# A 32x32 block inverse handed on inside SBUF, instead of through DRAM

## The chip, the cores and the metric

The kernel runs on one core of a Trainium2 chip. It uses all five engines: PE (TensorE, matrix products and transposes by product), DVE (VectorE), ACT (ScalarE), POOL (GpSimd) and SP (SyncE), whose instruction queue issues nearly all transfers between DRAM and the on-chip memories SBUF and PSUM. Each engine works through its own instructions strictly in order; an instruction that waits holds up everything behind it on that engine. The metric is the device time in microseconds (us) of one execution. Before the change it is 1262.1 us, the median of 3 runs (1261.81 to 1263.61).

## The reference, cut to what matters

The program is one layer of a hybrid encoder on 2048 positions of width 1024: RMS norm, one input projection, then two groups of heads in parallel, an output projection, and the residual sum. Group A (four heads of 128) is a gated delta rule run forwards and backwards; group B is windowed attention. The change lies in group A, in the part that inverts a unit lower triangular matrix for each chunk:

```python
    m = jnp.where(strict, jnp.einsum('bhncd,bhnsd->bhncs', k_beta, k) * decay, 0.0)
    eye = jnp.eye(c, dtype=q.dtype)
    t_inv = lax.linalg.triangular_solve(eye + m, jnp.broadcast_to(eye, m.shape),
                                        left_side=True, lower=True, unit_diagonal=True)
    u = jnp.einsum('bhncs,bhnse->bhnce', t_inv, v * beta[..., None])
    w = jnp.einsum('bhncs,bhnsd->bhncd', t_inv, k_beta * jnp.exp(g)[..., None])
    ...
    _, o = lax.scan(step, state0, xs)
```

The scan over chunks needs the inverses and is sequential: each step's state comes from the one before. The kernel uses chunks of 128 positions (16 per head and direction) instead of 64, which gives the same result by another split.

## The kernel before, in words

The first half of the program (up to some 690 us) makes the projections, the convolutions and the attention. The second half, `phase_b`, takes the four delta-rule heads one after another, and overlaps head h's scan with the preparation of head h+1:

- `pre_front(h)` makes, for all 16 chunks and both directions, the matrices m (with a product gh on PE, line 702, and a scaling on DVE into the tiles ma, line 711; for some heads these tiles lie in memory called xhi_h and xlo_h). Each group of four chunks is stored to DRAM (m_d, line 716). The memory of ma comes free only as earlier scans end: the front of head 2 ends behind the last steps of scan 0, that of head 3 behind those of scan 1. So from solve on, three pieces overlap: scan h, solve h+1, and then the end of front h+2.
- `solve(h)` reads back from m_d the 32x32 blocks on the diagonals (tiles X and L, lines 739 and 740): 2 directions x 16 chunks x 4 blocks are 128 blocks, one per SBUF partition, each with 32x32 numbers in the row. It inverts all of them at once by 31 steps of two DVE instructions (lines 749 and 753), and stores the result X to DRAM (x_d, line 754).
- `invert(h)` builds the 128x128 inverses from the block inverses, in four rounds `hi` of four chunks forwards and four backwards. For each round it loads two tiles xc from x_d (line 765): there a chunk's 128 rows lie on 128 partitions, with 4 chunks x 32 columns in the row. DVE transposes each 32x32 block of xc into xt (line 766); small copies place the blocks into block-diagonal tiles, iv (line 776, on DVE in round 0 and on DVE and POOL in the later ones) and ma (line 793, POOL). Then come five products on PE (pi, line 781) with ACT copies between.
- `scan(h)` is the sequential part: 16 steps for each of two directions, each with products pk, py, po on PE, copies on ACT and sums S, r, oacc on DVE.
- `fill` takes units of the output projection of group B (products pcs, lines 596 to 598) as work that depends on little and may stand anywhere in this half.

The order in which each engine runs its instructions is not that of the source text. At the end, `set_order` builds the graph of all instructions with a cost for each, plans it forwards and backwards several times, and pins the order of each engine's queue to the plan with the earliest planned end. So a change anywhere may move instructions everywhere. Tiles are taken from pools with a number of buffers: xc and xt have four each, L and X one each.

Of the kernel before, what the change touches and what calls it, by code (L numbers as in the profile page):

```python
# [7 lines left out]
F32 = mybir.dt.float32  # L8
F32R = mybir.dt.float32r
AF = mybir.ActivationFunctionType  # L10
# [5 lines left out]
P = 128  # L16
# [3 lines left out]
NCH = 16  # L20
# [526 lines left out]
def phase_b(ctx, wide, xe, ae, late, tc, t, ident, consts, hp, mix_dn, mix_sw, kq_d, v_d, zdn_d, zsw_d, dp, out):  # L547
    nc = tc.nc
    V, A, G, T = nc.vector, nc.scalar, nc.gpsimd, nc.tensor
    dma = nc.sync.dma_start  # L550

    def pool(name, bufs=1, stack=ctx, **kw):
        return stack.enter_context(tc.tile_pool(name=name, bufs=bufs, reuse_waits="tile", **kw))
# [63 lines left out]
    qa = pool("qa", stack=pre_stack)  # L617
# [5 lines left out]
    quads = [slice(32 * p, 32 * p + 32) for p in range(4)]  # L623
# [17 lines left out]
    def pre_front(h):  # L641
        H = {}
# [7 lines left out]
        mp = {}  # L650
        ma = H["ma"] = {}
        m_d = dp.tile([2, NCH, 4 * (32 * P + 32)], F32, tag="m_d", name=f"m_d{h}", bufs=2)
        x_d = dp.tile([2, NCH, P, 32], F32, tag="x_d", name=f"x_d{h}", bufs=2)
        for n, c4 in enumerate(FRONT):
            s4 = slice(4 * c4, 4 * c4 + 4)
            cs = slice(c4 * 512, (c4 + 1) * 512)
# [5 lines left out]
            for d in range(2):  # L662
# [12 lines left out]
                p = 3 - c4 if d else c4  # L675
# [22 lines left out]
            for c2 in range(2):  # L698
                gh = ps_g.tile([P, 2, 2, P], F32, tag="gh", name=f"gh{h}_{c4}_{c2}")
                for k in range(2):  # L700
                    c = 2 * c2 + k
# [3 lines left out]
                for k in range(2):  # L705
                    c = 2 * c2 + k
# [20 lines left out]
        for d in range(2):  # L727
            V.tensor_tensor(ck[:, d], bp[:, d], ekd[:, d, :, h], ALU.mult)

        H["solve"] = m_d, x_d, mp  # L730
        return H

    def solve(h, H):
        m_d, x_d, _ = H["solve"]
        L = qa.tile([P, 32, 32], F32, tag="L", name=f"L{h}")
        X = qa.tile([P, 32, 32], F32, tag="X", name=f"X{h}")
        lv = [m_d[d].rearrange("u (p y) -> (u p) y", p=4)[:, : 32 * P] for d in range(2)]
        lv = [a.rearrange("q (r x) -> q r x", x=P)[:, :, :32] for a in lv]
        dma(X[0:64], lv[0])
        dma(L[64:128], lv[1])  # L740
        x = X.rearrange("p r c -> p (r c)")
        V.tensor_copy(L[0:64], X[0:64].rearrange("p r c -> p c r"))
        G.memset(x, 0.0)
        G.memset(x[:, ::33], 1.0)
        for c in range(31):
            n = 31 - c
            tm = qa.tile([P, 256], F32, tag="tm", name=f"tm{h}_{c}")
            tv = tm[:, : n * (c + 1)].rearrange("p (r k) -> p r k", k=c + 1)
            V.tensor_tensor(
                tv, L[:, c + 1 :, c : c + 1].to_broadcast([P, n, c + 1]),  # L750
                X[:, c : c + 1, 0 : c + 1].to_broadcast([P, n, c + 1]), ALU.mult,
            )
            V.tensor_tensor(X[:, c + 1 :, 0 : c + 1], X[:, c + 1 :, 0 : c + 1], tv, ALU.subtract)
        dma(x_d.rearrange("d u (p r) c -> (d u p) (r c)", p=4), X.rearrange("p r c -> p (r c)"))

    def invert(h, H):
        _, x_d, mp = H["solve"]
        for hi in range(4):
            e1, p2, e2, e3 = (z[hi % len(z)] for z in zts)
            m = mp[hi]  # L760
            x0, x1 = {}, {}
            for d, c4 in ((0, hi), (1, 3 - hi)):
                xc = qb.tile([P, 4, 32], F32, tag="xc", name=f"xc{h}_{d}_{c4}", bufs=4)
                xt = qb.tile([P, 4, 32], F32, tag="xt", name=f"xt{h}_{d}_{c4}", bufs=4)
                dma(xc, x_d[d, 4 * c4 : 4 * c4 + 4].rearrange("u i c -> i u c"))
                V.transpose(xt.rearrange("p u c -> p (u c)"), xc.rearrange("p u c -> p (u c)"))
                x0[d], x1[d] = (xc, xt) if d == 0 else (xt, xc)
            g = qb.tile([P, 4, P], F32, tag="g", name=f"g{h}_{hi}", bufs=2)
            G.tensor_tensor(g, m[:, :, 0], m[:, :, 1], ALU.add)
            for s, a, b in zip("VGG" if hi else "VVV", (e1, e2, e3), ([0, 1, 0, 1], [1, 0, 1, 0], [0, 0, 1, 1])):  # L770
                xs = x1 if a is e2 else x0
                for q, k in zip(quads, b):
                    if s == "A":
                        A.activation(a[q, :, q], xs[k][q], AF.Copy)
                    else:
                        (V if s == "V" else G).tensor_copy(a[q, :, q], xs[k][q])

            def prod(j, lhs, rhs):
                o = ps_i[(hi + j) % 2].tile([P, 4, P], F32, tag="inv", name=f"pi{j}_{h}_{hi}")
                for c in range(4):  # L780
                    T.matmul(o[:, c], lhs(c), rhs(c), start=True, stop=True)  # L781
                return o

            def half(c):
                a = m[:, c].rearrange("p s i -> p (s i)")[:, :384].rearrange("p (e x) -> p e x", x=192)
                return a[:, :, :64]

            o = prod(0, lambda c: g[:, c], lambda c: e1[:, c])
            b1 = qb.tile([P, 4, P], F32, tag="b1", name=f"b1{h}_{hi}", bufs=2)
            A.activation(b1, o, AF.Copy, scale=-1.0)  # L790
            for d in range(2):
                for q in quads:
                    G.tensor_copy(m[q, :, 1 - d, q], x1[d][q])
            o = prod(1, lambda c: e2[:, c], lambda c: b1[:, c])
            for q, r in ((1, 0), (2, 3)):
                A.activation(e3[quads[q], :, quads[r]], o[quads[q], :, quads[r]], AF.Copy)
            o = prod(2, lambda c: b1[:, c], lambda c: e2[:, c])
            for r, q in ((0, 1), (1, 0), (2, 3), (3, 2)):
                A.activation(m[quads[r], :, 1 - r % 2, quads[q]], o[quads[r], :, quads[q]], AF.Copy)
            o = prod(3, lambda c: g[:, c], lambda c: e3[:, c])  # L800
            for d in range(2):
                A.activation(p2[halves[1 - d], :, halves[d]], o[halves[1 - d], :, halves[d]], AF.Copy, scale=-1.0)
            o = prod(4, lambda c: p2[:, c], half)
            for d in range(2):
                A.activation(m[halves[d], :, 1 - d, halves[1 - d]], o[halves[d], :, halves[1 - d]], AF.Copy)
# [90 lines left out]
    with tc.using_default_side("right"):  # L896
        zp = pool("zp", 4, stack=wide)
    kvs = {}
    H = pre_front(0)
    late(zp)  # L900
    solve(0, H)
    zts = [[const(f"iv{j}_{i}", [P, 4, P], None, qb) for i in range(2 - j % 2)] for j in range(4)]
    for grp in zts:
        for a in grp:
            G.memset(a, 0.0)
    invert(0, H)
    e1, e2 = (xe.tile([P, 8, 4, P], F32, tag=k, name=f"{k}_h") for k in ("xhi", "xlo"))
    mas = {1: e1[:, 0:4], 2: e1[:, 4:8], 0: e2[:, 4:8]}
# [8 lines left out]
    for h in range(3):  # L917
        scan(h, H)
        H = pre_front(h + 1)
        solve(h + 1, H)  # L920
        invert(h + 1, H)
# [19 lines left out]
    with tc.high_priority(-1000000):  # L941
        for k in range(2):
# [5 lines left out]
            for p in (0, 4, 2, 6, 5, 1, 3):  # L948
# [8 lines left out]
                a = (b11, b21, b22, b21, b11, b22, b12)[p]  # L957
# [459 lines left out]
```

## Time and profile before

| | |
|---|---|
| median of 3 runs | 1262.1 us |
| profiled execution: device time | 1270.01 us |
| profiled execution: span from first to last instruction | 1268.0 us |
| mean granted PE clock over the span | 0.989 |
| PE busy | 1210.5 us, 95% of the span |
| DVE busy | 953.7 us, 75% |
| ACT busy | 725.8 us, 57% |
| POOL busy | 529.2 us, 42% |

The profiled execution is 0.6% longer than the median; a sum of differences made in the trace is set against the trace's own time and then taken off the median. The share of busy time is an average over stages with different limits, so it says little by itself: what counts is, for each stage, which engine idles and which wait ends last there. The granted clock is the share of its full speed at which PE was allowed to run; a busy PE at clock 0.5 does half the work.

### The profile page before, as it was taken

The numbers are of one execution on the slowest core, as the hardware profiler recorded it, in microseconds if no ns is written. First come the engines' busy times: TensorE is split into PE (matmuls) and PEld (weight loads), VectorE is DVE, ScalarE is ACT, GpSimd is POOL, SyncE is SP. The second block draws the span as 40 slices with busy tenths as digits, with TensorE's granted clock in tenths as the row PEclk, the third lists the DMA queues.
The fourth block names the chain that finished last, engine by engine and source line by source line (L and its number), as shares of the span: only waits on it lengthen the run. The fifth ranks groups of instructions, "written<-read, shape, count | busy, mean of one in ns | idle before, by whom it ended". The sixth has DMA issues, their size and how long they took to land.

```text
span 1268.0 us, 22351 instructions
## 1 busy us (share of the span) xinstructions
PE 1210.5 (95%) x7018; PEld 1037.4 (82%) x7018; DVE 953.7 (75%) x2320; ACT 725.8 (57%) x2167; POOL 529.2 (42%) x845
## 2 busy tenths in 40 slices
PE   6999999999999999999999998999889899999898
PEld 5998888788889988887777777888789689888776
DVE  4523689999854379999995587698769779876765
ACT  6432476666534367766665438658557845685421
POOL 2243454763302276556422304613742441670541
PEclk9999999999999999999999999999889999999999
DMA  7553243513544434431016848967955875854785
GB/s 259 172 160 125 75 154 100 173 60 102 166 145 125 144 110 137 137 96 55 34 51 207 238 141 245 264 189 207 268 166 174 236 200 152 242 175 122 238 269 199
DMA packets 232294, 206.39 MB, mean 163 GB/s; under 512 B 49137, under 2 KB 181873, under 8 KB 232177
## 3 DMA queue, kind: packets, MB, share of 16 engines
q1 hardware_dynamic: 232176, 204.97, 53.0%
q8 instruction: 56, 0.92, 0.3%
q14 instruction: 62, 0.50, 0.1%
HBM read 139.84 MB, written 65.08 MB: 162 GB/s over the span
## 4 chain that ended last, share of the span: by engine, by line
PE 67%; DVE 13%; DMA 9%; ACT 4%; issue 3%; POOL 1%; SPq 1%; DVEq 0%; ACTq 0%; POOLq 0%
PE pf_c L199 5%; PE pf_c L201 5%; PE pf_c L200 5%; PE pf_z L199 4%; PE pf_z L200 4%; PE pf_z L201 4%; PE pi L781 3%; PE pq_q L212 2%; PE pq_q L211 2%; PE pt L390 2%; PE pq_q L210 2%; DMA xc<-x_d 2%; PE py L830 2%; PE po L839 2%; PE pcs L596 2%
## 5 line engine op out<-in xcount | busy, mean ns | idle before, releaser
L199 PE MATMUL pf_c<-xhi,wh_c 128*128 128x512 f32 x384 | 155.7, 405 | 0.8 <-DVE acc L269 0.8
L200 PE MATMUL pf_c<-xlo,wh_c 128*128 128x512 f32 x384 | 154.7, 403 | 0.0
L201 PE MATMUL pf_c<-xhi,wl_c 128*128 128x512 f32 x384 | 154.3, 402 | 0.0
L269 DVE SCALAR_TENSOR_TENSOR acc<-pf_c,cw,acc 128x512 f32<-128x512 f32 (+1 forms) x192 | 140.8, 742 | 2.6 <-POOL acc L259 0.7
L385 POOL TENSOR_SCALAR pr<-pr,st 128x384 f32<-128x384 f32 (+1 forms) x128 | 79.4, 639 | 98.0 <-DVE st L383 71.2
L394 ACT ACTIVATE ph<-pt 128x512 fp32r<-128x512 f32 x92 | 53.0, 595 | 60.5 <-PE pt L390 51.5
L376 ACT ACTIVATE pr<-pr,st 128x384 f32<-128x384 f32 (+1 forms) x128 | 76.2, 597 | 17.8 <-DVE st L372 17.4
L199 PEld LDWEIGHTS pf_c<-xhi,wh_c 128*128 128x128 f32 x384 | 72.5, 189 | 13.5 <-DVE acc L269 1.3
L201 PEld LDWEIGHTS pf_c<-xhi,wl_c 128*128 128x128 f32 x384 | 72.3, 188 | 12.9
L200 PEld LDWEIGHTS pf_c<-xlo,wh_c 128*128 128x128 f32 x384 | 72.4, 188 | 11.6
L835 ACT ACTIVATE yk<-py,ck 128x128 f32<-128x128 f32 x120 | 43.9, 366 | 62.0 <-PE py L830 61.2
L372 DVE CUSTOM_DVE_ANT_0 pr<-s,mask,sink 128x384 f32<-128x384 f32 (+1 forms) x128 | 73.4, 593 | 2.5 <-PE s L371 1.0
L211 PE MATMUL pq_q<-wh_q,xlo 128*128 128x256 f32 x256 | 72.1, 282 | 0.0
L212 PE MATMUL pq_q<-wl_q,xhi 128*128 128x256 f32 x256 | 71.9, 281 | 0.0
L210 PE MATMUL pq_q<-wh_q,xhi 128*128 128x256 f32 x256 | 71.4, 280 | 0.0
L390 PE MATMUL pt<-ident,pr 128*128 128x128 f32 x368 | 69.5, 274 | 1.8 <-DVE pl L395 1.1
L395 DVE TENSOR_TENSOR pl<-pt,ph 128x512 fp32r<-128x512 f32 x92 | 61.6, 681 | 6.1 <-ACT ph L394 5.6
L390 PEld LDWEIGHTS pt<-ident,pr 128*128 128x128 f32 x368 | 47.8, 140 | 20.4 <-DVE pl L395 4.4
L596 PE MATMUL pcs<-wohs,mhs 128*128 128x512 f32 x128 | 58.3, 456 | 4.4 <-ACT mhs L590 2.7
L692 POOL TENSOR_TENSOR nk<-ssk,pw 128x4 f32<-128x4 f32 x16 | 16.5, 1029 | 106.8 <-DVE ssk L691 106.6
L597 PE MATMUL pcs<-wohs,mls 128*128 128x512 f32 x128 | 56.1, 438 | 1.7 <-DVE mls L591 1.7
L598 PE MATMUL pcs<-wols,mhs 128*128 128x512 f32 x128 | 55.0, 429 | 0.0
(324 smaller groups left out, 4029.4 us busy)
## 6 DMA issues: line engine op xcount, KB each, us to landing
kqc<-kq_d SPq DMA_DIRECT2D x120, 128.0 KB, 3.1
ws_c<-wt SPq DMA_DIRECT2D x48, 256.0 KB, 3.5
xr<-x SPq DMA_DIRECT2D x16, 512.0 KB, 5.3
k_q<-kq_d SPq DMA_DIRECT2D x16, 512.0 KB, 5.6
mxs<-mix_sw SPq DMA_DIRECT2D x32, 256.0 KB, 3.7
xrs<-x SPq DMA_DIRECT2D x32, 256.0 KB, 3.7
part<-xrs SPq DMA_DIRECT2D x32, 256.0 KB, 2.6
xrd<-part SPq DMA_DIRECT2D x32, 256.0 KB, 4.1
```

The costliest lines, as they stand in the source:

```text
L199: T.matmul(ps, hi[:, k, cs], xhi[b][:, k], start=(k == 0), stop=False)
L200: T.matmul(ps, hi[:, k, cs], xlo[b][:, k], start=False, stop=False)
L201: T.matmul(ps, lo[:, k, cs], xhi[b][:, k], start=False, stop=(k == KC - 1))
L210: T.matmul(ps[:, :n], xh, hi[:, k, :n], start=(k == 0), stop=False)
L211: T.matmul(ps[:, :n], xl, hi[:, k, :n], start=False, stop=False)
L212: T.matmul(ps[:, :n], xh, lo[:, k, :n], start=False, stop=(k == KC - 1))
L269: V.scalar_tensor_tensor(av, ps[:, lo:], cw[:, i, k : k + 1], av, ALU.mult, ALU.add)
L372: V.tensor_tensor_reduce(pr[j][:, :n], ps[:, :n], mask[:, lo * P : hi * P], 1.0, sink[:, hh : hh + 1], ALU.add, ALU.min, accum_out=nm[:, j ...
L376: A.activation(pr[j][:, :n], pr[j][:, :n], AF.Exp, bias=nm[:, j : j + 1], scale=-1.0, accum_out=den[:, j : j + 1])
L385: G.tensor_scalar(pr[j][:, :n], pr[j][:, :n], den[:, j : j + 1], 1.0, ALU.mult, ALU.mult)
L390: T.transpose(pt[:, j], pr[j][:, (kb - lo) * P : (kb - lo + 1) * P], ident)
L596: T.matmul(ps, mh[:, k], wh[:, k], start=(k == 0), stop=False)
```

## The change

The block inverses no longer go through DRAM. After `solve`, one DVE instruction transposes all 32x32 blocks within groups of 32 partitions into a new tile Y, which uses the memory of L: what was (block number on the partition; row, column in the row of memory) becomes (column on the partition; block number, row). In `invert`, each tile xt is then put together by four copies of 32 partitions x 128 numbers, from one quarter of the partitions to another, two on DVE and two on ACT; one DVE transpose makes xc from xt, where before it made xt from xc. The transfers of lines 754 and 765, one store and eight loads per head, are gone. `set_order` plans the whole program anew.

```diff
-        x_d = dp.tile([2, NCH, P, 32], F32, tag="x_d", name=f"x_d{h}", bufs=2)
...
     def solve(h, H):
...
-        dma(x_d.rearrange("d u (p r) c -> (d u p) (r c)", p=4), X.rearrange("p r c -> p (r c)"))
+        Y = H["Y"] = qa.tile([P, 8, 4, 32], F32, tag="L", name=f"Y{h}")
+        V.transpose(Y.rearrange("p u q r -> p r (u q)"), X)
 
     def invert(h, H):
...
             for d, c4 in ((0, hi), (1, 3 - hi)):
                 xc = qb.tile([P, 4, 32], F32, tag="xc", name=f"xc{h}_{d}_{c4}", bufs=4)
                 xt = qb.tile([P, 4, 32], F32, tag="xt", name=f"xt{h}_{d}_{c4}", bufs=4)
-                dma(xc, x_d[d, 4 * c4 : 4 * c4 + 4].rearrange("u i c -> i u c"))
-                V.transpose(xt.rearrange("p u c -> p (u c)"), xc.rearrange("p u c -> p (u c)"))
+                b = 32 * (2 * d + c4 // 2)
+                for p, q in enumerate(quads):
+                    a = Y[b : b + 32, 4 * (c4 % 2) : 4 * (c4 % 2) + 4, p]
+                    if "VAVA"[p] == "A":
+                        A.activation(xt[q], a, AF.Copy)
+                    else:
+                        V.tensor_copy(xt[q], a)
+                V.transpose(xc.rearrange("p u c -> p (u c)"), xt.rearrange("p u c -> p (u c)"))
```

The planned order shows what moves. In the names the first digit behind the letters is the head (gh3 is head 3; xc2_0_0 is head 2, direction 0, group 0), and the last number only tells buffers apart; line numbers behind the change are up to 6 higher. On DVE, at the end of solve 2, these rows stand around the first use of the block inverses of head 2, before:

```order
L711 SCALAR_TENSOR_TENSOR xhi_h_9049<-gh3_0_1_13145,bp3_12946,v2_q_7736 128x2x128
L693 RECIPROCAL ssk3_12944<-ssk3_12944 128x4
L766 STREAM_TRANSPOSE xt2_0_0_11967<-xc2_0_0_11966 128x128
L776 COPY iv0_0_8769<-xc2_0_0_11966 32x4x32
L711 SCALAR_TENSOR_TENSOR ma3_3_13102<-gh3_0_1_13145,bp3_12946,v2_q_7736 128x2x128
...
L766 STREAM_TRANSPOSE xt2_1_3_11971<-xc2_1_3_11970 128x128
L694 TENSOR_TENSOR bp3_12946<-beta_4894,ssk3_12944 128x2x4
L776 COPY iv0_0_8769<-xt2_1_3_11971 32x4x32 x2
L711 SCALAR_TENSOR_TENSOR ma3_3_13102<-gh3_3_0_13205,bp3_12946,v2_q_7736 128x2x128
```

and after:

```order
L710 SCALAR_TENSOR_TENSOR ma3_3_13173<-gh3_0_1_13216,bp3_13018,v2_q_7736 128x2x128
L693 TENSOR_TENSOR bp3_13018<-beta_4894,ssk3_13016 128x2x4
L574 TENSOR_TENSOR wols1_13310<-woss1_3_13323,wohs1_13309 128x512
L771 COPY xt2_0_0_12015<-Y2_12012 32x128
L710 SCALAR_TENSOR_TENSOR ma3_3_13173<-gh3_3_0_13276,bp3_13018,v2_q_7736 128x2x128
...
L710 SCALAR_TENSOR_TENSOR xhi_h_9073<-gh3_3_0_13276,bp3_13018,dc3_3_1_13242 128x2x128
L591 TENSOR_TENSOR mls1_1_13353<-mxs1_1_13350,mhs1_1_13352 128x512
L772 STREAM_TRANSPOSE xc2_0_0_12014<-xt2_0_0_12015 128x128
L782 COPY iv0_0_8769<-xt2_1_3_12022 32x4x32
```

Before, the scaling of gh3_0_1 and gh3_3_0 (the front of head 3) stands behind the transpose that waits for the load; after, it stands ahead of it.

On PE, at the same place, before:

```order
L702 MATMUL gh3_0_1_13145<-k2_q_7735 128x256 x2
L719 MATMUL trv3_3_13229<-ident_66,k2_q_7735 128x128 x4
...
L702 MATMUL gh3_3_0_13205<-k2_q_7735 128x256 x2
...
L781 MATMUL pi0_2_0_11988<-iv0_0_8769,g2_0_11974 128x128 x2
...
L781 MATMUL pi1_2_0_12003<-b12_0_11993,iv2_0_8772 128x128 x4
L702 MATMUL gh3_3_1_13216<-k2_q_7735 128x256 x2
```

and after:

```order
L701 MATMUL gh3_0_1_13216<-k2_q_7735 128x256 x2
L718 MATMUL trv3_3_13300<-ident_66,k2_q_7735 128x128 x4
...
L701 MATMUL gh3_3_0_13276<-k2_q_7735 128x256 x2
...
L701 MATMUL gh3_3_1_13287<-k2_q_7735 128x256 x2
...
L598 MATMUL pcs1_1_13358<-wols1_13310,mhs1_1_13352 128x512
L787 MATMUL pi0_2_0_12042<-iv0_0_8769,g2_0_12028 128x128 x4
```

Between trv3_3 and the first product pi of head 2 stand 6 filler products pcs before and 24 after, and gh3_3_1, which stood behind that pi, now stands ahead of it.

On SP, behind the end of solve 2, up to the loads for solve 3 (lines 739 and 740), before:

```order
L716 DMA m_d3_12949<-xhi_h_9049 128x4x128
L765 DMA xc2_0_0_11966<-x_d2_11360 128x4x32
L572 DMA woss1_3_13252<-wout 128x512
L765 DMA xc2_1_3_11970<-x_d2_11360 128x4x32
L593 DMA xrs0_1_13262<-x 128x512
L765 DMA xc2_0_1_12033<-x_d2_11360 128x4x32
L819 DMA kqc2_1_3_12360<-kq_d2_89 128x2x128
L765 DMA xc2_1_2_12037<-x_d2_11360 128x4x32
L819 DMA kqc2_0_4_12380<-kq_d2_89 128x2x128
L716 DMA m_d3_12949<-xlo_h_9050 128x4x128
```

and after:

```order
L715 DMA m_d3_13021<-xhi_h_9073 128x4x128
L825 DMA kqc2_1_3_12432<-kq_d2_89 128x2x128
L583 DMA mxs1_1_13350<-mix_sw1_72 128x512
L825 DMA kqc2_0_4_12452<-kq_d2_89 128x2x128
L825 DMA kqc2_1_4_12473<-kq_d2_89 128x2x128
L572 DMA woss1_3_13323<-wout 128x512
L593 DMA xrs0_1_13333<-x 128x512
L715 DMA m_d3_13021<-xlo_h_9074 128x4x128
```

The four loads xc that stood between two stores of head 3's matrices are gone, and other transfers have moved up.

More of the change, by code (lines that the diff above doesn't have):

```diff
@@ L728, in pre_front @@
             V.tensor_tensor(ck[:, d], bp[:, d], ekd[:, d, :, h], ALU.mult)
-        H["solve"] = m_d, x_d, mp
+        H["solve"] = m_d, mp
         return H
     def solve(h, H):
-        m_d, x_d, _ = H["solve"]
+        m_d = H["solve"][0]
         L = qa.tile([P, 32, 32], F32, tag="L", name=f"L{h}")
@@ L753, in solve @@
             V.tensor_tensor(X[:, c + 1 :, 0 : c + 1], X[:, c + 1 :, 0 : c + 1], tv, ALU.subtract)
-        dma(x_d.rearrange("d u (p r) c -> (d u p) (r c)", p=4), X.rearrange("p r c -> p (r c)"))
+        Y = H["Y"] = qa.tile([P, 8, 4, 32], F32, tag="L", name=f"Y{h}")
+        V.transpose(Y.rearrange("p u q r -> p r (u q)"), X)
     def invert(h, H):
-        _, x_d, mp = H["solve"]
+        Y, mp = H["Y"], H["solve"][1]
         for hi in range(4):
```

## Prediction

> **What bounds the kernel now.** I read the page's busy shares first, then PE's idle time by stage, then the chain of work that ended last, then DVE's instructions at the places where the chain shows the removed transfers.
>
> ```profile
> span 1268.0 us, 22351 instructions
> ...
> PE 1210.5 (95%) x7018; PEld 1037.4 (82%) x7018; DVE 953.7 (75%) x2320; ACT 725.8 (57%) x2167; POOL 529.2 (42%) x845
> ```
>
> PE is the bound overall: only 57.5 us of the span are free of it. The stages (span; busy time of PE, PEld, DVE, ACT, POOL; granted clock; share of the DMA engines) show where these lie:
>
> ```profile
> 32.00:640.00 608.00, 604.44 (x3391) 515.93 (x3391) 460.01 (x966) 340.19 (x804) 281.12 (x438) 1.00 0.37 118
> 760.00:880.00 120.00, 111.41 (x724) 97.52 (x723) 96.55 (x295) 85.09 (x332) 48.47 (x81) 0.99 0.78 225
> 880.00:960.00 80.00, 69.93 (x451) 63.22 (x450) 60.09 (x177) 48.33 (x177) 40.03 (x74) 0.91 0.75 215
> 960.00:1080.00 120.00, 112.03 (x753) 99.80 (x752) 102.21 (x328) 76.54 (x298) 40.59 (x75) 0.97 0.67 194
> 1080.00:1180.00 100.00, 95.23 (x685) 84.88 (x683) 75.53 (x217) 67.55 (x241) 48.48 (x77) 1.00 0.62 182
> ```
>
> The first 640 us have nothing to give. From 760 to 1180 us, where the four heads are solved and scanned, PE idles 31 us, and for part of the rest it runs at a lower clock. The chain of work passes through the removed transfers there, at head 1:
>
> ```profile
> 882.43 6.82 DMA x_d<-X
> 889.27 4.05 DMA xc<-x_d
> ...
> 896.11 2.06 PE pi L781 x8
> ```
>
> and at head 2:
>
> ```profile
> 989.96 6.23 DMA x_d<-X
> ...
> 996.21 7.61 DMA xc<-x_d
> ```
>
> That is 10.9 and 13.8 us of pure transport. But how much of it is lost? Four stretches answer, one per head, each from the end of the solve (the last X of line 753) to the end of the first four copies iv, which the first products pi need:
>
> ```profile
> 768.02:783.22 15.20, 14.09 (x74) 11.31 (x73) 9.05 (x28) 11.22 (x50) 7.45 (x14) 1.00 0.96 280
> 882.00:895.98 13.98, 9.66 (x56) 7.76 (x54) 11.00 (x35) 10.90 (x54) 5.46 (x9) 0.99 0.96 292
> 988.79:1005.86 17.07, 11.43 (x71) 9.26 (x70) 12.09 (x43) 12.87 (x66) 6.98 (x10) 0.97 0.90 258
> 1076.89:1087.65 10.76, 10.76 (x80) 9.67 (x79) 7.36 (x25) 8.46 (x35) 3.60 (x6) 1.00 0.83 234
> ```
>
> PE idles 1.1, 4.3, 5.6 and 0.0 us in them: heads 0 and 3 hide the transport behind late gates and scan 2. And at heads 1 and 2 DVE and ACT are busy for 11 to 13 us of the 14 and 17, with the ends of a scan and of a front. So the transport is worth no more than what it holds up beyond that work.
>
> **The change part by part.** *New work.* The prices come from these rows of single tiles (min/median/max in ns; the group of line 742 has its mean behind the bar):
>
> ```profile
> L776 DVE COPY iv<-xc x48: 171/218/1206, 779.7 to 1110.2; 32x128 f32<-32x128 f32 x48
> L766 DVE STREAM_TRANSPOSE xt<-xc x32: 270/311/314, 779.4 to 1109.8; 128x128 f32<-128x128 f32 x32
> L742 DVE COPY L<-X 64x1024 f32<-64x1024 f32 x4 | 4.4, 1111 | 0.2 <-DMA X<-m_d 0.2
> L799 ACT ACTIVATE ma<-pi x40: 249/268/270, 790.5 to 1149.9; 32x128 f32<-32x128 f32 x40
> L765 SPq DMA_DIRECT2D xc<-x_d x32: 359/500/2141, 774.7 to 1105.2; - x32
> ```
>
> The transpose of 1024 numbers per partition is in no row. It lies between the strided copy of as many numbers (1.11 us) and eight small transposes (8 x 0.311 = 2.5 us); I take 1.3, near the copy, since a long instruction pays its start once. The 16 DVE copies per head cost as the copies iv do, 16 x 0.218 = 3.5 us; the eight transposes stay. DVE: 4.8 us per head, 19.2 in all. ACT: 16 x 0.268 = 4.3 us per head, 17 in all. A copy between partition quarters is in no row either; the bounds are the shortest copy, 0.171, and a small transpose, 0.311.
>
> *The stretches to the first pi.* By the order, ahead of the fourth iv stand 7, 6, 5 and 8 new copies on DVE and the large transpose: 2.4 to 3.1 us. If DVE never waited, the stretches would last 9.05+2.8 = 11.9, 11.00+2.6 = 13.6, 12.09+2.4 = 14.5 and 10.5 us. Against 15.2, 14.0, 17.1 and 10.8 that is 3.3, 0.4, 2.6 and 0.3 shorter. At head 1 the order also moves most of the last scalings ma behind the copies iv, 0.48 us each; I count 1.2 us for head 1, and 2.4 for head 2, where DVE stood still for 3.25 us and made PE's gh wait:
>
> ```profile
> 1003.84 0.31 DVE L766 STREAM_TRANSPOSE xt<-xc 128x128 f32<-128x128 f32 x1 [3.25 <-DMA xc<-x_d]
> ...
> 1004.69 1.99 PE L702 MATMUL gh<-k_q 128*128 128x256 f32 x4 [2.57 <-DVE ma L711]
> ```
>
> In the order for the change the scalings behind that transpose come ahead of it, and 24 fillers instead of 6 stand before the first pi of head 2, so nothing new waits for xt there; late next are the copies on ACT, which sit among the squares jko. Head 0: of 3.3 us only PE's idle 1.1 can count; I take 0.5. Head 3: 0. Bounds over the four: 0, if DVE waits as long for PE and ACT as it did for the load, to 11, all of PE's idle time there. Taken: 4.1.
>
> *The clock.* Behind the two idle places PE runs slower:
>
> ```profile
> 890.00:895.00 5.00, 2.48 (x12) 1.73 (x10) 3.31 (x12) 3.71 (x18) 1.09 (x4) 1.00 1.10 320
> 895.00:900.00 5.00, 3.20 (x13) 2.94 (x14) 4.73 (x18) 1.23 (x4) 4.08 (x9) 0.56 0.91 238
> 900.00:905.00 5.00, 5.00 (x30) 4.56 (x29) 2.88 (x10) 3.90 (x14) 2.95 (x11) 0.76 0.89 244
> 1000.00:1005.00 5.00, 1.27 (x4) 0.79 (x5) 1.69 (x8) 1.59 (x6) 2.95 (x4) 0.98 0.84 196
> 1005.00:1010.00 5.00, 5.00 (x20) 4.19 (x20) 3.94 (x15) 3.87 (x18) 2.52 (x7) 0.68 0.81 196
> ```
>
> and the wait between them:
>
> ```profile
> 896.11 2.05 PE L781 MATMUL pi<-iv,g 128*128 128x128 f32 x8 [3.64 <-DVE iv L776]
> ```
>
> Lost: 0.44 x 3.2 + 0.24 x 5.0 = 2.6 us and 0.32 x 5.0 = 1.6. With shorter gaps I take half back, 2.1 (bounds 0 and 4.2). The Trainium skill, "TensorE: Matmul & The Clock Gate", section "Why this matters for your kernels", says to leave PE no gaps of more than about 3 us, as one idle window halves its clock. The trace agrees: the gap before the first pi of head 1 was 3.64 us, and the clock behind it 0.56. By that rule a gap of half the length would give back all 4.2, and the forecast would be 2 us lower; the sum keeps the half.
>
> *SP and the DMA engines.* 36 issues go, 32 x 0.500 and four stores like them, 18 us on a queue that is in order, and the loads fall into stretches where the DMA share is 0.83 to 0.96 already (last column but one of the stretches above). Behind both inversions PE waits for transfers that came through that crowd:
>
> ```profile
> 924.46 6.88 DMA xrs<-x
> ...
> 930.00:935.00 5.00, 1.76 (x11) 1.52 (x10) 3.55 (x8) 1.53 (x4) 2.69 (x3) 0.81 0.26 88
> 935.00:940.00 5.00, 5.00 (x20) 4.52 (x20) 3.33 (x11) 0.90 (x3) 4.06 (x12) 0.50 0.36 104
> ...
> 1030.00:1035.00 5.00, 3.37 (x22) 2.53 (x20) 3.18 (x6) 2.48 (x8) 3.31 (x7) 1.00 0.89 291
> 1035.00:1040.00 5.00, 4.96 (x22) 4.29 (x22) 2.75 (x13) 1.44 (x5) 2.95 (x11) 0.66 0.43 137
> ```
>
> Idle 3.2 and 1.6 us, clock 0.3 + 2.5 and 1.7: 9.3 us. The removed loads are not the cause of it all, so I take 3.7; bounds 0 and 9.3.
>
> *What it costs elsewhere.* Of DVE's 4.8 us per head 2.2 lie outside the stretches, in scans where DVE is up to 85% busy (102.21 of 120 in one stage). PE is full there, so most is covered; if it is not, DVE's scan sums S and r come later, and pk behind them. I charge 0.5 per head, 2.0. ACT's 4.3 per head is covered by its idle time and charged at nothing; if that cover goes, the products' copies b and iv come later, up to 1 us per head. Y lies in L's memory, so the load of L for the next solve must now wait for the last copies into xt. Before, the last xt of head 1 and that load stood thus:
>
> ```profile
> 913.48 0.30 DVE L766 STREAM_TRANSPOSE xt<-xc 128x128 f32<-128x128 f32 x1
> ```
>
> ```profile
> 914.49 3.90 SPq L740 DMA_DIRECT2D L<-m_d  x1
> ```
>
> That is close. If the copies come late, SP stands, and behind it the loads kqc for scan 1; but they come some us sooner than the loads did, so I charge nothing and keep 3 us for the range.
>
> Sum: 4.1 + 2.1 + 3.7 - 2.0 = 7.9, call it 8 us. The profiled execution would go from 1270 to 1262, its span from 1268 to 1260; that execution lies 8 us above the median, so the median goes from 1262.1 to 1254. The measurement can tell about 0.2%, 2.5 us, from no change.
>
> **The rivals.** *The gain is larger:* each head's front, solve and scan hang on the one before, and a head that starts earlier frees the next one's front, store and solve. For it speaks that head 3's gh stood behind the wait at 1003.84; against it that PE has its other work to do whatever the order. All of the stretches' 11 at two thirds, all of the clock and of the crowd at two thirds: 7.3 + 2.8 + 6.2 - 0 = 16, which with 2 us for the earlier front gives 1244.
>
> *Nothing is gained:* DVE had 11.00 us to do out of 13.98 anyway, and the planned order puts 25 to 36 rows between the end of a solve and the first pi, as before. Then only a few us of the crowd are left, set against the 2 charged: 1261.
>
> *DVE becomes the bound:* slower. Place: from the end of solves 1 and 2 through the first rounds of the inversions, where DVE is the engine that makes iv, S and r. If DVE's waits for PE and ACT stay (3 to 5 us per stretch) and its new 4.8 us per head land on the path as often as it is busy, 0.85 x 19.2 = 16 us are added, less 6 for crowd and clock: 1272. It decides once a stretch gets longer than 14 or 17 us. For it: 102 busy us of 120. Against: PE was idle, not late, at these places. The Trainium skill, "VectorE: DVE Perf Modes", section "Two Vector instructions with no wait between them", speaks for this rival: an instruction whose input or output starts in another group of 32 partitions than the last one's starts only when all earlier ones have finished. The new copies do that nearly every time, so none would overlap its neighbour. The trace agrees that neighbours may overlap otherwise: of these two rows the second starts 0.23 us behind the first, which takes 0.31; so an estimate for the rule's price is 0.08 us for each of 64 copies, 5 us more on DVE.
>
> ```profile
> 893.35 0.31 DVE L766 STREAM_TRANSPOSE xt<-xc 128x128 f32<-128x128 f32 x1 [1.01 <-DMA xc<-x_d]
> 893.58 0.17 DVE L776 COPY iv<-xc 32x128 f32<-32x128 f32 x1
> ```
>
> *The new order is worse elsewhere:* the plan changes from the first projections on, where PE has 3.6 us free of 608 and can only lose, and at the end. No row prices it; I set 5 us against a gain half as large: 1263.
>
> **How the numbers follow.** Forecast (1249 to 1259): 0.45. Larger gain: 0.20. Nothing: 0.13. DVE bound: 0.13. Order: 0.09. Faster by over 0.2%, under 1259.6, are the first two, 0.03 of the order's case and 0.02 of the empty one: 0.70. Slower, over 1264.6, are the DVE case, 0.04 of the order's and 0.02 of the empty one: 0.19. Within 0.2% is left with 0.11. The range, 1243 to 1267, leaves out the best third of the larger gain and most of the DVE case.
>
> **What would show it.** The waits of DVE on xc and of SP on the store are gone. In the stretch of head 2, PE's idle falls below 3 us and the clock behind it stays above 0.8; at head 1 PE's idle is about 3. Y takes 1.1 to 2.5 us, a copy about 0.22. From 905 to 940 transfers land sooner than in 6.9 us. DVE is 19 us busier, ACT 17. I am wrong if the stretches do not shorten, if PE's idle time only moves to the scans, or if the first 760 us change by more than 3 us.

## The result, and the profile after

The change is slower: 1276.6 us (median of 3 runs, 1276.1 to 1277.3) against 1262.1, a ratio of 1.0112 with a 95% interval of 1.0089 to 1.0135. I had forecast 1254. The profiled execution took 1276.14 us, close to its median; that of before, 1270.01, lay 8 us above its own, so the two traces show only 6 of the 14 us. Where both are compared below, I go by places and not by the spans. Three runs each are few: in the later series the kernel before had medians of 1262.7 to 1265.0 us, with single executions from 1257 to 1275, so the loss may be nearer to 12 us than to 14. Every ratio below is taken within its own series.

The page of the change begins:

```profile
span 1274.4 us, 22447 instructions
...
PE 1211.8 (95%) x7018; PEld 1032.3 (81%) x7018; DVE 984.4 (77%) x2388; ACT 745.6 (59%) x2231; POOL 535.6 (42%) x845
```

PE does the same 7018 products, busy 1.3 us longer; DVE is 30.7 us busier and ACT 19.8. The stages of the change (span; busy time of PE, PEld, DVE, ACT, POOL; clock; DMA share):

```profile
32.00:640.00 608.00, 604.22 (x3380) 513.76 (x3378) 458.52 (x959) 338.56 (x797) 282.65 (x434) 1.00 0.37 119
700.00:760.00 60.00, 55.22 (x249) 43.54 (x250) 38.23 (x100) 24.18 (x85) 10.98 (x10) 1.00 0.71 200
760.00:880.00 120.00, 111.73 (x711) 98.27 (x710) 106.08 (x314) 86.43 (x330) 44.66 (x78) 0.99 0.71 206
880.00:960.00 80.00, 71.55 (x478) 62.32 (x477) 71.09 (x206) 58.97 (x218) 45.78 (x79) 0.98 0.77 219
960.00:1080.00 120.00, 108.53 (x725) 95.37 (x724) 105.15 (x330) 80.20 (x310) 40.22 (x74) 0.96 0.60 177
1080.00:1180.00 100.00, 94.83 (x682) 84.67 (x680) 81.03 (x229) 72.06 (x257) 47.07 (x77) 1.00 0.52 163
```

and of before, the one stage not shown yet:

```profile
700.00:760.00 60.00, 58.33 (x265) 46.72 (x264) 41.35 (x111) 24.72 (x87) 11.06 (x10) 1.00 0.66 186
```

Two things are to be seen. From 700 to 760 us PE does 3.1 us less, although no changed instruction stands there: the first transpose Y starts at 776.3. And in the two middle stages DVE is busy 71 of 80 and 105 of 120 us (before: 60 and 102). From 880 to 960 us PE does 1.6 us more than before, at a clock of 0.98 instead of 0.91; from 960 to 1080 it does 3.5 us less. The copies of L, one per head, tell where the time goes: they stand 4.2, 5.2, 3.4 and 11.5 us later than before (before: 729.8, 818.4, 923.1, 1026.6), and the end 6.4 later. So most is lost between the third of these copies and the fourth, and some of it comes back behind that. The new work itself, single tiles of the change (min/median/max in ns):

```profile
L769 ACT ACTIVATE xt<-Y x64: 290/308/312, 778.4 to 1125.3; 32x128 f32<-32x128 f32 x64
L771 DVE COPY xt<-Y x64: 204/218/1333, 778.4 to 1119.9; 32x128 f32<-32x128 f32 x64
L754 DVE STREAM_TRANSPOSE Y<-X x4: 1960/1984/2070, 776.3 to 1083.6; 128x1024 f32<-128x1024 f32 x4
```

The four stretches from the end of a solve to the fourth copy iv, in the change:

```profile
774.81:785.76 10.95, 10.42 (x50) 8.30 (x48) 10.61 (x27) 8.29 (x30) 5.75 (x9) 1.00 0.85 256
887.29:899.53 12.24, 10.65 (x63) 8.59 (x61) 11.99 (x37) 11.70 (x48) 5.99 (x8) 1.00 0.90 264
998.43:1016.40 17.97, 10.18 (x41) 6.51 (x41) 13.36 (x38) 11.72 (x52) 4.62 (x7) 0.86 0.67 188
1083.56:1097.68 14.12, 12.77 (x86) 11.08 (x86) 12.27 (x35) 12.23 (x48) 6.29 (x10) 1.00 0.66 216
```

Heads 0 and 1 got shorter, by 4.3 and 1.7 us, heads 2 and 3 longer, by 0.9 and 3.4: together 1.7 us shorter. Head 1 ended with DVE busy in 11.99 of 12.24 us. What happened at head 2 stands in DVE's queue (start, us, instruction, idle time before it and what ended that):

```profile
1005.35 0.16 DVE L693 TENSOR_TENSOR bp<-beta,ssk 128x8 f32<-128x8 f32 x1
1008.01 0.69 DVE L574 TENSOR_TENSOR wols<-woss,wohs 128x512 fp32r<-128x512 f32 x1 [2.50 <-ACT wohs L573]
1008.62 0.21 DVE L771 COPY xt<-Y 32x128 f32<-32x128 f32 x1
...
1011.47 0.46 DVE L710 SCALAR_TENSOR_TENSOR ma<-gh,bp,v_q 128x256 f32<-128x256 f32 x1
1011.86 0.46 DVE L710 SCALAR_TENSOR_TENSOR xhi_h<-gh,bp,dc 128x256 f32<-128x256 f32 x1
```

and in the chain of work, behind that wait:

```profile
1002.36 4.97 DMA woss<-wout
1007.35 0.64 ACT wohs L573
```

The planned order had put a row of a filler (line 574, which splits a weight of the output projection of group B) ahead of the first copy into xt, as the second order listing under "The change" shows. Its weight came late, DVE stood still for 2.5 us, and the copies, the front's scalings and PE's gh behind them all moved back:

```profile
1012.38 2.07 PE L701 MATMUL gh<-k_q 128*128 128x256 f32 x4 [3.13 <-DVE xhi_h L710]
...
1016.30 0.77 PE L596 MATMUL pcs<-wohs,mhs 128*128 128x512 f32 x1 [1.85 <-DVE xhi_h L710]
```

So one wait on a transfer (xc, 3.25 us) went, and another (a weight, 2.5 us) stands in its place, at which the clock (last column but two) fell again, where before it was 0.68 and then back at 1.00:

```profile
1010.00:1015.00 5.00, 2.07 (x4) 1.17 (x4) 4.29 (x16) 4.75 (x23) 1.14 (x4) 0.63 0.47 119
1015.00:1020.00 5.00, 3.70 (x9) 2.97 (x10) 4.70 (x16) 1.55 (x5) 3.05 (x6) 0.50 0.57 184
```

### The profile page after: what moved, and what is told of

The parts are those of the page before. It is cut to its first block, busy times and chain, and to the rows that moved or that the text cites. A ratio compares the mean times of both kernels' runs of the same rounds, so it can differ in the third digit from the quotient of the medians.

```text
span 1274.4 us, 22447 instructions
## 1 busy us (share of the span) xinstructions
PE 1211.8 (95%) x7018; PEld 1032.3 (81%) x7018; DVE 984.4 (77%) x2388; ACT 745.6 (59%) x2231; POOL 535.6 (42%) x845
```

## The experiments

Three theories. *Order:* the order planned anew is worse than the one of before, whatever it carries. *Work:* the new rows on DVE (or ACT) fall on the path. *Memory:* Y lies in L's memory, and the next head's load waits. To tell order from work, some kernels have their order pinned: a table gives each instruction its place, and the queues are filled from it instead of the plan. "Old order" below is the order of before for all rows that both kernels have; new rows stand where the old ones stood.

```diff
-    end, begin, queue = best
+    place = zlib.decompress(base64.b85decode(PLACE))
+    place = [int.from_bytes(place[2 * k : 2 * k + 2], "little") for k in range(n)]
...
+    while heap:
+        k = heapq.heappop(heap)[1]
+        if eng[k]:
+            queue[eng[k]].append(k)
...
```

All ratios are to the kernel before on the same chip, with 95% intervals.

**Each work in the other's order.** The change's work in the old order:

> The changed kernel's work, but every engine's queue in the order that the kernel before had; the new rows take the places of the old ones (Y where the store stood, the four copies just ahead of the place of the transpose). If the newly planned order made the change slow, this run is faster than before: 1250 to 1258 us. If DVE's 30 us of added work are the cause, the old order does not help: 1270 to 1280. If the cause is that the load of L waits for the last reader of Y, the loads stand in SP's queue at their old places and must stand there longer: 1264 to 1275, with L's copies 3 to 10 us later than before and nothing else late.

The work of before, with its transfers, in the change's order:

> The kernel before's work, with the transfers, but every engine's queue in the order planned for the change; the store stands where Y stood, the loads right behind. If the planned order is the cause: 1275 to 1285 us, as slow as the change or slower, since the transport is on the path as well. If DVE's added work or the wait of L's load for Y's readers is the cause, both are absent here: 1262 to 1267.

Measured: 1.0148 (1.0112 to 1.0185; 1282.6 us) and 1.0257 (1.0214 to 1.0300; 1297.4). The old order does not rescue the new work, against the theory of order alone; whether it is any worse for it than the change's own order (1.0112), the intervals do not tell. The new order costs the old work 2.6%, against work alone. Neither theory is the whole.

**What a replan costs by itself.** The planner's constants moved by 1 ns; the work is the same.

```diff
-LAG = {"PE": 205, "DVE": 140, "Activation": 160, "Pool": 120, "SP": 2400}
+LAG = {"PE": 205, "DVE": 141, "Activation": 160, "Pool": 120, "SP": 2400}
```

The kernel before with this, with DVE at 139, and with ACT (`Activation`) at 161:

> The kernel before with no change of work: the planner reckons one ns more for DVE's latency, and so plans another order. If a replan by itself costs (the order of before is an uncommonly good one), this run is slower than 1262 by 5 to 12 us. If DVE's work or L's memory is the cause of the change's loss, a replan is worth nothing in the mean: 1259 to 1265.

> The kernel before, work unchanged, DVE's latency in the planner one ns less: a second order drawn by chance. If the order of before is an uncommonly good one, this is 1268 to 1278 us again, and the first replan was no accident. If that replan was an accident, 1260 to 1266.

> The kernel before, work unchanged, ACT's latency in the planner one ns more: a third order. If an order drawn by chance costs the kernel before some 8 us in the mean, 1266 to 1278 us; otherwise 1260 to 1266.

Measured: 1.0081 (1.0046 to 1.0116), 1.0049 (1.0026 to 1.0072), 1.0109 (1.0062 to 1.0156). With no work changed, each replan is 6 to 14 us slower. The loss begins where the change's did: PE's busy time from 700 to 760 us in the first of them is

```profile
700.00:760.00 60.00, 55.17 (x244) 44.22 (x243) 35.57 (x92) 25.87 (x89) 11.08 (x10) 0.97 0.68 196
```

The change with DVE at 139, ACT at 161, and POOL at 119:

> The change, work as it is, DVE's latency in the planner one ns less. If the change's loss is the loss of a good order and its work is worth nothing either way, this lies among the replans of before, 1265 to 1278 us. If the hand-over saves the 8 us that I forecast and only the order hid it, the change's orders lie 8 us under those of before: 1260 to 1268. If its work costs (DVE, or L's memory), they lie above: 1278 to 1290.

> The change, work as it is, ACT's latency in the planner one ns more. As for the other replan of the change: 1265 to 1278 us if the work is worth nothing, 1260 to 1268 if the hand-over saves, 1278 to 1290 if its work costs.

> The change with POOL's latency in the planner one ns less: the shortest of some 90 plans (1195.4 us by the planner's own reckoning, the same as that of the kernel before, where the change's own plan has 1201.3). If the loss is that before has a picked order and the change a chance one, this is 1260 to 1268 us. If the planner's reckoning tells little, it is one more chance order: 1266 to 1280.

Measured: 1.0098 (1.0060 to 1.0137), 1.0023 (0.9992 to 1.0054), 1.0071 (1.0042 to 1.0100). With the change's own 1.0112 the mean of four orders is 1.0076; that of before's three replans is 1.0080. Among orders drawn by chance the change is worth nothing that these few draws could show. The shortest plan, the last of the three, came out in the middle of the four, so the planner's own reckoning is a weak guide to the good order.

**Y's memory.** Y with memory of its own, in two orders (in the second POOL's constant is 110):

```diff
-        Y = H["Y"] = qa.tile([P, 8, 4, 32], F32, tag="L", name=f"Y{h}")
+        Y = H["Y"] = qa.tile([P, 8, 4, 32], F32, tag="Y", name=f"Y{h}")
...
-            b1 = qb.tile([P, 4, P], F32, tag="b1", name=f"b1{h}_{hi}", bufs=2)
+            b1 = qb.tile([P, 4, P], F32, tag="b1", name=f"b1{h}_{hi}", bufs=1)
...
-                    kqc = rp.tile([P, 2, P], F32, tag=f"kqc{d}", name=f"kqc{nm}", bufs=4)
+                    kqc = rp.tile([P, 2, P], F32, tag=f"kqc{d}", name=f"kqc{nm}", bufs=3 + d)
```

> The change with memory of its own for Y, so that the load and the copy of L for the next head need not wait for the copies into xt; to make room, b1 has one buffer instead of two and the kqc of direction 0 three instead of four. The planner plans anew. If the wait for Y's readers is the cause: 1258 to 1266 us, and L's copy for head 3 stands as early as before, within 3 us of 1027. If DVE's work is the cause: 1274 to 1280. If the order is the cause, this is one more draw of an order, 1262 to 1280, whatever L's copies do.

> The change with memory of its own for Y, in another order (POOL's latency in the planner ten ns less). If memory of its own is worth something apart from the order, this lies below the replans of the change with Y in L's memory (1.0023 to 1.0112 of before), at 1260 to 1268 us. If the first run of it was one good draw, 1268 to 1278.

and, in the old order, copies that read a constant instead of Y:

```diff
-                    a = Y[b : b + 32, 4 * (c4 % 2) : 4 * (c4 % 2) + 4, p]
+                    a = ident[b : b + 32].rearrange("p (u c) -> p u c", u=4)
```

> As the change's work in the old order (1282.6 us), but the copies into xt read a constant tile instead of Y, so the load of L for the next head waits for nothing new and ACT's copies don't wait for Y; the block inverses do not reach the products, so the output is not the reference's. If the wait for Y's readers is what makes the change slow in the old order: 1262 to 1270. If DVE's and ACT's work is: 1278 to 1285.

Measured: 1.0028 (1.0006 to 1.0051), 1.0100 (1.0063 to 1.0138), and 1.0155 (1.0128 to 1.0181) where the same with Y had 1.0148. The first looked like a hit, but in a second order it did not repeat, and two orders cannot tell it from chance; in the pinned order the wait is worth nothing that could be measured. The trace of the change had pointed at it: SP's load of L for head 3 starts right behind the last copy out of Y (1031.31, 0.22 us, on DVE), and the copy of L for that head 11.5 us later than before.

```profile
1024.78 0.61 SPq L738 DMA_DIRECT2D X<-m_d  x1
...
1030.60 0.32 SPq L897 DMA_DIRECT2D mix_dn<-zt  x1
1031.60 0.60 SPq L739 DMA_DIRECT2D L<-m_d  x1
```

But in the same order with no Y at all (the last experiment below) the two loads start within a microsecond of these, and the copy of L in both at 1038.1:

```profile
1025.54 0.61 SPq L738 DMA_DIRECT2D X<-m_d  x1
1026.20 3.11 SPq L593 DMA_DIRECT2D xrs<-x  x1
...
1031.39 0.60 SPq L739 DMA_DIRECT2D L<-m_d  x1
```

Without Y the load stands behind the other rows that the plan had put between the two loads. Y can account for the 0.7 us of idle SP ahead of it in the first fence, and for nothing of the 11.5. This reason falls: two things that end together are not cause and effect.

**The price of each part, in the old order.** The transport left out (`xz` is a constant tile), and then the transport kept and the new work added as a dummy: all of it, and each part alone.

```diff
-        dma(x_d.rearrange("d u (p r) c -> (d u p) (r c)", p=4), X.rearrange("p r c -> p (r c)"))
...
-                xc = qb.tile([P, 4, 32], F32, tag="xc", name=f"xc{h}_{d}_{c4}", bufs=4)
+                xc = xz[0]
...
-                dma(xc, x_d[d, 4 * c4 : 4 * c4 + 4].rearrange("u i c -> i u c"))
```

> The kernel before in its own order, with the store and the eight loads per head simply left out: the block inverses are replaced by one constant tile, so the output is not the reference's. No new work stands in their place. It measures what the transport is worth in that order. By the forecast's sum for the transport (4.1 + 2.1 + 3.7): 1252 to 1258 us. If the order of before hides it: 1261 to 1267.

```diff
+        Y = qa.tile([P, 8, 4, 32], F32, tag="L", name=f"Y{h}")
+        V.transpose(Y.rearrange("p u q r -> p r (u q)"), X)
...
+                    if "VAVA"[p] == "A":
+                        A.activation(xe_[q], ident[b : b + 32], AF.Copy)
+                    else:
+                        V.tensor_copy(xe_[q], ident[b : b + 32])
```

> The kernel before in its own order, transfers kept, and the change's new work added as a dummy: per head one transpose of 128x1024 into L's memory and 16 copies each on DVE and ACT into a scratch tile, from a constant, so nothing waits for their data; nobody reads the results. It measures the price of the work alone. By the forecast (2 us charged): 1263 to 1268. If DVE is the bound: 1278 to 1290. As one order for another work, planned without these rows: 3 to 8 us.

> The kernel before in its own order, transfers kept, with the 64 copies of 32x128 on ACT alone added as a dummy (20 us of ACT's time). I charged ACT at nothing. If that holds: 1261 to 1265 us. If the copies stand in the chain of the inversion, whose every product needs a copy on ACT: 1268 to 1275. The three parts of the work together cost 18 us.

> The kernel before in its own order, transfers kept, with the 64 copies of 32x128 on DVE alone added as a dummy (18 us of DVE's time). If DVE's work falls on the path about as often as DVE is busy (85%): 1274 to 1280. If it is covered, as I charged it (2 us): 1262 to 1266. If only rows beside POOL's work count, which hold a copy up to 1.3 us: 1266 to 1270.

> The kernel before in its own order, transfers kept, with the transpose of 128x1024 alone added behind each solve (4 x 2 us on DVE). It stands where DVE waits for the load of xc anyway, so it should be covered: 1262 to 1265 us. If DVE has no such room: 1268 to 1271.

| old order, pinned | ratio (95%) | us of 1262 |
|---|---|---|
| transport left out | 0.9902 (0.9879 to 0.9926) | -12.4 |
| all new work as a dummy | 1.0146 (1.0118 to 1.0173) | +18.4 |
| ACT's copies alone | 1.0008 (0.9985 to 1.0031) | +1.0 |
| DVE's copies alone | 1.0130 (1.0096 to 1.0164) | +16.4 |
| Y alone | 1.0038 (1.0018 to 1.0058) | +4.8 |
| the change's work, no transport | 1.0148 (1.0112 to 1.0185) | +18.7 |

ACT's copies cannot be told from free (-1.9 to +3.9 us), as I had charged them. DVE's are not: 64 copies, 21.2 us of DVE's time, cost 16.4, and Y, which I expected to be covered by the wait for xc, 4.8 of its 8.

```profile
L770 DVE COPY xe<-ident 32x128 f32<-32x128 f32 x64 | 21.2, 331 | 1.1
```

So DVE is on the path most of the time there, for all that PE is "full". One place is the scan's sum r. PE's waits for it ahead of the product py (total, number, longest, in us), for before, for DVE's copies alone and for the change's work in the old order:

```profile
PE py L830 <- DVE r L823: 1.8, 4, 0.8
PE py L835 <- DVE r L828: 4.9, 4, 2.8
PE py L836 <- DVE r L829: 9.4, 9, 2.5
```

These waits name a place and not the whole price: with ACT's copies alone they are 3.2 us, at 1.0 us of cost. How far the four heads are spread shows the delay too. The copies of L, one per head, with the start of the first and of the last, for DVE's copies alone:

```profile
L742 DVE COPY L<-X x4: 1095/1106/1109, 732.7 to 1033.5; 64x1024 f32<-64x1024 f32 x4
```

for ACT's copies alone:

```profile
L742 DVE COPY L<-X x4: 1101/1110/1116, 730.3 to 1024.4; 64x1024 f32<-64x1024 f32 x4
```

and with the transport left out:

```profile
L742 DVE COPY L<-X x4: 1103/1108/1108, 731.3 to 1013.5; 64x1024 f32<-64x1024 f32 x4
```

That is 300.8, 294.1 and 282.2 us for three heads; before had 296.8 (729.8 to 1026.6).

The last two lines with all the work are the lesson: +18.4 with the transport, +18.7 without. The 12.4 us that the transport is worth are there only while nothing stands in its place. With the dummy, DVE's waits for the loads xc are all but gone (0.3 us against 8.3 before): the new work fills them. In the hand-over itself they come back as waits for ACT's copies. DVE's waits ahead of its small transpose, before and with the change's work in the old order:

```profile
DVE xt L766 <- DMA xc<-x_d: 8.3, 8, 3.2
DVE xc L772 <- ACT xt L769: 9.2, 12, 2.8
```

So in this order the transport's gain is not there beside the new work. That the two lines agree to 0.3 us is chance, since their difference is uncertain by some 6 us. In the change's own order the waits for ACT's copies are 0.5 us.

**All copies on ACT.** If DVE's copies cost and ACT's don't, the copies belong on ACT:

```diff
-                    if "VAVA"[p] == "A":
+                    if "AAAA"[p] == "A":
```

> The change's hand-over with all four copies of a tile on ACT and none on DVE, in the old order, the ACT copies put 2.5 us of planned time ahead of the place of the transpose. The parts measured in that order: transport left out -11 us, Y +5, ACT's copies +1 for 64 and so +2 for 128. If they add up: 1256 to 1261 us, faster than before. If leaving out the transport is worth nothing as soon as new work stands in its place, as in the change's work in the old order: 1267 to 1273, and DVE waits for xt from ACT where it waited for xc before.

Measured: 1.0170 (1.0147 to 1.0192), 1283.7 us. A miss: the parts do not add up. As a dummy nobody waits for ACT's copies; as the hand-over, the transpose into xc, iv and pi need them. At head 3, the one place looked at, Y was ready at 1082.7 (DVE: from 1080.78, 1.96 us), and ACT's queue, in order, came to its copies late:

```profile
1083.52 0.37 ACT L841 ACTIVATE yk<-py,ck 128x128 f32<-128x128 f32 x1 [2.64 <-PE py L836]
...
1087.32 0.83 ACT L805 ACTIVATE ma<-pi 32x128 f32<-32x128 f32 x3
1088.17 1.28 ACT L769 ACTIVATE xt<-Y 32x128 f32<-32x128 f32 x4
...
1090.19 1.26 ACT L769 ACTIVATE xt<-Y 32x128 f32<-32x128 f32 x4
...
1095.41 1.26 ACT L769 ACTIVATE xt<-Y 32x128 f32<-32x128 f32 x4
```

5.4 us after Y the first copies start, and those of the second round 12.7 us after it, though ACT stood still for 2.64 us around Y's end. Where I had put these rows in the old order was too late for them at this head. An order planned for copies on ACT alone was not run, so it stays open whether they could be had cheaply.

**The change's own order, without its work.** This splits the change's loss where it happened:

```diff
-        Y = H["Y"] = qa.tile([P, 8, 4, 32], F32, tag="L", name=f"Y{h}")
-        V.transpose(Y.rearrange("p u q r -> p r (u q)"), X)
...
-                xt = qb.tile([P, 4, 32], F32, tag="xt", name=f"xt{h}_{d}_{c4}", bufs=4)
+                xt = xz[0]
```

> The change in its own planned order, with the new work left out: no transpose Y, no copies into xt, and no transport either; a constant tile takes the place of the block inverses, so the output is not the reference's. It splits the change's own 1276 us. In the old order the hand-over left out gave 1251.5 us. If a chance order costs some 10 us whatever the work, this is 1259 to 1264 us, and the new work costs 12 to 17 us in its own order too. If the order planned for the work hides most of it, so that only the order is slow, 1270 to 1275. If the order is as good as the old one and the work is all: 1249 to 1255.

Measured: 1.0028 (1.0003 to 1.0054); 1267.8 us, a little above the first case of the expectation. Its three heads take 301.8 us, against 282.2 in the old order with the same work:

```profile
L741 DVE COPY L<-X x4: 1049/1084/1117, 736.3 to 1038.1; 64x1024 f32<-64x1024 f32 x4
```

So one account of the change, each step a measured pair, in us of 1262:

| step | ratio | us |
|---|---|---|
| transport left out, old order | 1 to 0.9902 | -12.4 |
| the order of the change in place of the old, no hand-over at all | 0.9902 to 1.0028 | +15.9 |
| the new work, in the change's order | 1.0028 to 1.0112 | +10.6 |
| sum | | +14.1 |

Each step is uncertain by some 4 us, and the 10.6 are the new work together with the waits for it, since a constant tile is there at once. The split depends on the way taken. The six kernels side by side, in us against the kernel before:

| | with the transport | no hand-over | with the new work |
|---|---|---|---|
| old order | 0 | -12.4 | +18.7 |
| the change's order | +32.4 | +3.5 | +14.1 |

Read downwards, the change's order costs 32.4 and 15.9 for work it was not planned for; for its own work the difference is -4.5, within its uncertainty of some 5 us. Read across, the new work in place of the transport costs 18.7 in the old order and saves 18.3 in the change's. So no share of the 14 us belongs to the order alone. What holds on either way is that the new work, against nothing in its place, costs 10.6 or 31.0. Which rows carry the 10.6 in the change's own order was not found: there PE's waits for r ahead of py are 1.3 us, less than before. No kernel that computes the result beat the one before.

## Why the prediction was wrong

- *The transport's worth* (4.1 + 2.1 + 3.7 = 9.9 us) was near in size for the old order, 12.4 by the run that left it out; in the change's order it was 28.9 (1.0028 to 1.0257). It was wrong to book it as a gain beside the new work: in the old order the same gap was filled by that work or held by its waits.
- *What it costs elsewhere* is the first step that failed. I charged DVE 0.5 us per head, since PE is full where DVE is 85% busy. The new work costs 10.6 us in the change's order; in the old one DVE's copies alone cost 16.4. PE being full on average says nothing of single sums that its next product needs in time: in the old order PE's waits for r grew from 1.8 to 9.4 us. In the change's own order they did not, and there the place stays open. ACT at nothing was right (1.0 us) for copies that nobody waits for.
- *The order* is the second: I put it among the rivals with 5 us and a chance of 0.09, because no row priced it, and left it out of the sum. A replan of the unchanged kernel cost 6 to 14 us, and with no hand-over at all the change's order was 15.9 slower than the old one; its share in the change itself cannot be parted from the work's. My own condition, "if the first 760 us change by more than 3 us", was met: L was copied 4.2 us later at head 0 (734.0 against 729.8). Not all of that need be the order, since in the pinned old order this copy stood anywhere from 729.1 to 734.2.
- *Prices.* Y took 1.98 us, not 1.3, inside its bounds of 1.1 to 2.5. A copy on DVE took 0.218 in the median, as taken, but 0.286 in the mean, 18.3 us for all 64, where I had 14; on ACT 0.308, not 0.268. DVE was to get 19 us busier and got 30.7, of which Y and the copies are 26; ACT 17 and got 19.8.
- *The stretches* were to shorten by 4.1 and shortened by 1.7: more than taken at heads 0 and 1 (4.3 for 0.5, 1.7 for 1.2), the other way at heads 2 and 3. At head 1 PE idled 1.6 us, better than the 3 forecast; at head 2 7.8 instead of under 3. PE's idle time in the four was 11.1 us and is 11.3.
- *The clock* behind head 2 was 0.63 and 0.50, where I wanted over 0.8. Reckoned as in the prediction, in stretches of 5 us, the loss behind head 1 fell from 2.6 to 1.5 us (clock 0.89 and 0.76) and behind head 2 rose from 1.6 to 3.4: of the 4.2 us nothing was given back.
- *The crowd.* Behind inversion 1 the chain of work still goes through one slow load, as long as the 6.88 us before, but PE hardly idled behind it:

```profile
916.35 6.90 DMA zcs<-zsw_d
925.00:940.00 15.00, 13.96 (x102) 12.60 (x101) 11.55 (x32) 11.48 (x39) 13.46 (x27) 1.00 0.67 195
```

  Before, PE idled 3.2 us from 930 to 940 us and lost 2.8 by the clock; here it idles 1.0 from 925 to 940 at full clock. At this place the term's 3.7 us were there, but the stage from 960 to 1080 us, with head 2, does 3.5 us less than before.

- *L's load*, which I charged at nothing and kept 3 us for, cost nothing that could be found.
- *The rival "DVE becomes the bound"* (1272 us) had the mechanism of the work in the old order, and its size: 0.85 x 19.2 = 16 us, against 16.4 for DVE's copies and 18.4 for all. The agreement is partly luck, since the work was 26 us and not 19.2. I gave it 0.13 because PE was idle and not late at these places, which did not bear on the rest of the scan. It was not the whole: a replan without new work cost 6 to 14 us.

## What to carry to other kernels

Where a planner sets the order, first measure what a replan without any change of work costs (here 0.5 to 1.1%); a change that is worth less cannot be read from one build. Pinning the order prices the parts, but for that order alone: here the same exchange cost 18.7 us in one order and saved 18.3 in the other. Before a transfer is replaced by instructions, ask whether the engine that runs them has room at that very place in its queue: here the removed wait was filled by the work that removed it, or came back as a wait for it. And a part that is free as a dummy is not free once somebody waits for it.

## What the runs showed of the hardware

A DVE copy of 32x128 from SBUF to SBUF takes 0.22 us, but beside a tensor operation of POOL it can take more than five times as long. In DVE's queue of the change:

```profile
905.30 1.22 DVE L771 COPY xt<-Y 32x128 f32<-32x128 f32 x1
```

and in POOL's:

```profile
905.17 2.49 POOL L672 TENSOR_TENSOR v_q<-v_q,dmask 128x512 f32<-128x512 f32 x2 [2.71 <-DMA v_q<-gr_d]
```

One of these two POOL instructions takes 1.27 us in the median, so the copy, 0.13 us behind the first one's start, ends about with it. At four places copies into xt of the change are held so, which is why their mean is 0.286 us:

```profile
L771 DVE COPY xt<-Y 32x128 f32<-32x128 f32 x64 | 18.3, 286 | 1.6 <-POOL iv L782 0.2
```

The Trainium skill, "SBUF — State Buffer", section "Who interferes with whom", says that a DVE copy in its two-port mode and a POOL instruction exclude each other from a port pair that they share: the later one waits until the first has finished. The rows agree with the waiting; that these copies run in that mode no row shows.

The transpose of 1024 numbers per partition took 1.98 us, nearly twice the 1.11 us of a strided copy of as many: this long DVE transpose was not paced like a copy.
